# The first norm's second half of scale and shift ahead of chunks 1 and 2 on TensorE, and free banks for layer 1's values

## The chip, the cores and the metric

The kernel runs on one core of a Trainium2 chip. A core has five engines with queues of their own: TensorE (PE: matmuls and transposes, from SBUF into the 8 PSUM banks), VectorE (DVE), ScalarE (ACT), GpSimd (POOL) and SyncE (SP), which here issues the loads of the weights. The metric is the device time of one execution in microseconds (us), median of several runs; less is better.

## The reference, cut to what matters

A decoder trunk of 2 layers on 256 tokens with a model width of 1024. Every sub-layer normalises its input and scales and shifts it by a projection of the condition c:

```
for i in range(DEPTH):                                  # DEPTH = 2
    mod = jax.nn.silu(c) @ ada_w[i] + ada_b[i]          # 1024 x 6144
    sh_a, sc_a, g_a, sh_f, sc_f, g_f = jnp.split(mod[:, None, :], 6, axis=-1)
    h = rms_norm(x, attn_norm[i]) * (1.0 + sc_a) + sh_a
    if i % 2 == 0:
        y = sparse_mixer(h, ...)   # MoBA (8 heads) beside NSA (8 heads, 2 groups)
    else:
        y = diff_mixer(h, ...)     # differential attention, 8 heads
    x = x + g_a * y
    h = rms_norm(x, ffn_norm[i]) * (1.0 + sc_f) + sh_f
    x = x + g_f * ((jax.nn.silu(h @ w_gate) * (h @ w_up)) @ w_down)

def diff_mixer(h, ...):
    q, k, v = jnp.split(h @ w_in, [qk_w, 2 * qk_w], axis=-1)   # 1024 columns each
    # rms_norm and rotary embedding of q and k; v goes on as it is
    # a = softmax(q0 k0) - lam * softmax(q1 k1);  o = a @ v, per head
    return (rms_norm(o, out_norm) * (1.0 - lam_init)) @ w_out
```

## The kernel before, in words

**Products.** Each fp32 product is done as three matmuls of a rounded and a remaining part: `mm3` issues hi x hi, hi x lo and lo x hi into one PSUM bank. A weight comes by DMA in units of 512 KB into one of 5 `raw` buffers (`raw_tile`); `split` (L186 to 188) writes `hi` on ACT (L187) and `lo` on DVE (L188) into one of 5 ring buffers. The activations are kept transposed and split as `bigT` buffers, in two halves of 512 of the 1024 input features each (`hts[0]`, `hts[1]`), both for all 256 tokens.

**Order.** A scheduler sets the order on each engine by its own estimate of times; it prefers what was written first. `weave` mixes several generators of instructions by their weights. `hold` is a list from which each weight unit takes an entry: its split then stands behind the named instructions. `chain`, if it is not empty, ties each matmul behind the one before it, the first behind the name in the list. Neither costs a semaphore wait of its own. SP issues the loads in the order of the program.

**Banks.** `bank_tiles` are the 8 PSUM banks; `banks(...)` gives groups their banks (ACC for accumulations, others for scores, transposes and outputs), and `bank(*group)` takes the next of a group.

**The first norm** (`nsa_first`, L920 and after). `ada_first(0)` multiplies the condition (`cs`) with the first half of scale and shift, 8 loads of 512 KB; the row goes into a bank, is copied out on ACT (L383), transposed back into columns by PE (L387) and finished on DVE (L354, L356: `col`). `out_half(0)` transposes the first half of the normalised x (`xn`, L406, in `norm_T`) and scales, shifts and splits it on ACT (L422, L187) and DVE (L415, L188) into the first `bigT`. The first projection has three chunks of 512, 512 and 280 columns in the banks (0,1), (2,3) and (4,5). `ada_first(1)` takes the second half of scale and shift by 8 loads, whose tiles come from the list `FIRST` and, where that is used up, from the `raw` ring; then come `out_half(1)`, `half(n, 0)` for the three chunks (the matmuls on the first `bigT`), and `half(n, 1)` (those on the second).

**Layer 1** (`diff_proj`, `diff_heads`). Part 0 projects K and Q for the first four heads (`proj2`: kTn, qT), then the values (`proj` with `prep_v`: vm). Part 1 does the same for the other four (kTm, qTm), and runs woven with the heads of part 0. In a head the scores (`kTn,qT`) go into banks 4 and 5, a softmax row is made on DVE (L890) and ACT (L892), two of them are combined on DVE (L1246 to L1250), transposed (L909) and multiplied with the values (`vm,pT`).

Of the kernel before, what the change touches and what calls it, by code (L numbers as in the profile page):

```python
# [17 lines left out]
P = 128  # L18
# [3 lines left out]
NT = S // P  # L22
# [10 lines left out]
RND = 12582912.0  # L33
WARM = 0
NQ = 2


def BOTH(i, j, n):
# [6 lines left out]
def weave(*gens):  # L45

    live = [[g, n, 0] for g, n in gens]
    while live:
        live.sort(key=lambda e: (e[2] + 0.5) / e[1])
        e = live[0]  # L50
        try:
            next(e[0])
            e[2] += 1
        except StopIteration:
            live.remove(e)
# [8 lines left out]
def tile_trunk(ctx: ExitStack, tc: tile.TileContext, x, c, positions, ada_w, ada_b, attn_norm, ffn_norm,  # L64
# [4 lines left out]
    V, A, T, G = nc.vector, nc.scalar, nc.tensor, nc.gpsimd  # L69
# [6 lines left out]
    bank_tiles = [pp.tile([P, 512], F32, name=f"bank{i}") for i in range(8)]  # L76
    bank_at = {}

    def bank(*group):
        i = bank_at.get(group, 0)  # L80
        bank_at[group] = i + 1
        return bank_tiles[group[i % len(group)]]

    ACC, SC, TR, OT, CB = [], [], [], [], []
# [16 lines left out]
    def tmp(shape, tag, bufs, dt=F32):  # L101
        return sp.tile(shape, dt, name=nm(tag), tag=tag, bufs=bufs)
# [8 lines left out]
    chain = []  # L111
# [20 lines left out]
    ident = cp.tile([P, P], F32, name="ident")  # L132
# [58 lines left out]
    hold = []  # L191
# [6 lines left out]
    def raw_tile():  # L198
        return wp.tile([P, 1024], F32, name=nm("raw"), tag="raw", bufs=5)

    FIRST = [("nkv", 2), ("nkv", 2), ("tok4", 2), ("tok4", 2), ("qTm", 1), ("kTm", 1), ("vm", 1), ("kTn", 1),
             ("mod", 2), ("mod", 2), ("qT", 1), ("ada_acc", 2), ("araw", 2), ("araw", 2), None]

    def first_raw():

        if not FIRST:
            return raw_tile()
        at = FIRST.pop(0)
        if at is None:
            return bias  # L210
        if at[0] == "araw":
            return wp.tile([P, 1024], F32, name=nm("araw"), tag="araw", bufs=2)
        return tmp([P, 1024], *at)

    R5 = ("ring",) * 5
    units = dict(first=[], cyc=list(R5), n=0)
# [186 lines left out]

    def norm_T(t, f, xn, b):
        for k in range(4):
            T.transpose(out=b[:, k * P:(k + 1) * P], in_=xn[:, f * 512 + k * P:f * 512 + (k + 1) * P], identity=ident)  # L406

    def norm_out(i, js, t, f, b, ht, behind=None):

        sh, sc = cols[(i, js)], cols[(i, js + 1)]  # L410
        hf = tmp([P, 4, P], "w2k", 4)
        for k in range(4):
            kk = f * 4 + k
            if k % 2:
                v = V.tensor_scalar(out=hf[:, k, :], in0=b[:, k * P:(k + 1) * P], scalar1=sc[:, kk:kk + 1],  # L415
                                    scalar2=sh[:, kk:kk + 1], op0=ALU.mult, op1=ALU.add)
                if behind:
                    after(v, behind)
                ks = slice(k - 1, k + 1)
                h = split(hf[:, ks], ht[0][:, ks, t * P:(t + 1) * P], ht[1][:, ks, t * P:(t + 1) * P])  # L420
            else:
                A.activation(out=hf[:, k, :], in_=b[:, k * P:(k + 1) * P], func=AF.Identity, scale=sc[:, kk:kk + 1],  # L422
                             bias=sh[:, kk:kk + 1])
        return h[1], h[0]
# [82 lines left out]
        yield  # L507
        yield from late(*its)

    def proj(hts, w, c0, n, done):  # L510

        bs = [bank(*ACC) for _ in range(NT)]
        for u in range(4):
            wu, = proj_units(w, c0, n, [u])
            for t in range(NT):
                proj_mm(hts, bs[t][:, 0:n], t, u, wu)
            yield
        yield from done(bs)
# [230 lines left out]
    def prep_v(v):  # L749
        def done(bs):  # L750
            for t in range(NT):
                A.activation(out=v[t], in_=bs[t], func=AF.Copy)
            yield
        return done
# [167 lines left out]
    def nsa_first(hts):  # L922

        w = sp_w_in[0]
        spec = [(1536, 512, (0, 1)), (2048, 512, (2, 3)), (2560, 280, (4, 5))]
        xn = [tmp([P, D], "xn", 2) for _ in range(NT)]

        def out_half(f):
            for t in range(NT):
                b = bank_tiles[6 + t if f or not t else 5]  # L930
                norm_T(t, f, xn[t], b)
                lst[:] = [norm_out(0, 0, t, f, b, hts[f])]

        lst = []

        def half(n, f, wus=None):
            c0, w_, bi = spec[n]
            for e in range(2):
                u = 2 * f + e
                wu = wus[e] if wus else proj_units(w, c0, w_, [u])[0]  # L940
                for t in range(NT):
                    proj_mm(hts, bank_tiles[bi[t]][:, 0:w_], t, u, wu)

        def stats():
            for t in range(NT):
                ss = tmp([P, 2], "ss2", 2)
                for e in range(2):
                    sumsq_x(t, e, ss, xn[t])
                norm_stats(t, ss, xn[t])

        setup_rope()
        ada_first(0, bank_tiles[4], bank_tiles[7])
        stats()
        out_half(0)
        hold[:] = [None] + [lst[0]] * 5
        wus = [proj_units(w, c0, w_, (0, 1)) for c0, w_, _ in spec]
        ada_first(1, bank_tiles[7], bank_tiles[7])
        out_half(1)
        for n in range(3):
            half(n, 0, wus[n])  # L960
        V.memset(bias, 0.0)
        dma(bias[0:12, :], ada_b.rearrange("i (j n) -> (i j) n", j=6))
        setup_small(lst[0])
        for n in range(3):
            half(n, 1)
            yield [bank_tiles[k] for k in spec[n][2]]
# [233 lines left out]
    def diff_proj(hts, part, st):  # L1200
        w = diff_w_in[0]
        qT = tmp([P, 1024], "qT" if part == 0 else "qTm", 1).rearrange("p (k n) -> p k n", k=4)
        kT = tmp([P, 1024], "kTn" if part == 0 else "kTm", 1).rearrange("p (k n) -> p k n", k=4)
        if part == 0:
            vt = tmp([P, NT, 512], "vm", 1)
            v = [vt[:, t, :] for t in range(NT)]
        else:
            v = [tmp([P, 1024], "nkv", 2)[:, 0:512] for _ in range(NT)]
        nrs = tmp([P, NT, 8], "nrs", 2)
        st[part] = (qT, kT, v, nrs)  # L1210
        cs_ = (1024 + part * 512, part * 512)
        dones = (prep_k(kT, 7, fc(5)), prep_q(qT, nrs, 6, 1.0))
        if part == 0:
            yield from proj2(hts, w, cs_, dones)
        else:
            for c0, d in zip(cs_, dones):
                yield from proj(hts, w, c0, 512, d)
        yield from proj(hts, w, 2048 + part * 512, 512, prep_v(v))

    def diff_heads(part, st, oh, ol):  # L1220
        qT, kT, v, nrs = st[part]
# [51 lines left out]
    def first(g, n):  # L1273
        for _ in range(n):
            if next(g, g) is g:
                return
            yield

    def late(*gens):
        for g in gens:  # L1280
            yield from g
# [6 lines left out]
    on = pair()  # L1288
    om = pair()
    nh = nsa_heads(*on)  # L1290
    weave((late(np_, first(nh, 6)), 22), (moba_proj(hts), 20), (ada(0, 2, pin=True), 11))
    hts = new_hts()
    banks([], [0, 1, 2], [4, 5], [6, 7])
    settle()
# [62 lines left out]
```

## Time and profile before

| | |
|---|---|
| median of 3 runs | 755.86 us (754.24 to 756.33) |
| profiled execution | 762.01 us, span 759.9 us |
| mean granted TensorE clock | 0.967 of full speed |
| PE busy | 712.9 us, 94% of the span |
| DVE busy | 505.6 us, 67% |
| ACT busy | 415.1 us, 55% |
| DMA | 159.41 MB, mean 210 GB/s |
| chain that ended last | PE 75%, DVE 8%, DMA 7%, ACT 6% |

The profile is of one execution, which took 6.15 us longer than the median. Busy shares are over the whole span; what holds up the kernel at one place is read from the rows of that place: a row names the engine, the line, the names and shapes of the tiles, and in square brackets how long the engine had stood idle before it and what released it. PEclk is the clock that TensorE was granted, as a share of its full speed.

### The profile page before, as it was taken

How to read it: one execution, taken by the hardware profiler on the slowest of the kernel's cores; microseconds unless marked ns; L12 is line 12 of the kernel's file. 1: busy time of each engine (PE TensorE's matmuls, PEld its weight loads, DVE VectorE, ACT ScalarE, POOL GpSimd, SP SyncE). 2: the span in 40 equal slices, each digit the busy share in tenths (PEclk: the TensorE clock that was granted, in tenths of full speed). 3: DMA queues.
4: the chain of work that ended last, by engine and by line, in shares of the span. 5: the costliest groups of instructions: out<-in, count | busy, mean ns of one | idle time of the engine just before them, and what ended most of it. 6: DMA issues, size and time to landing. Idle time of an engine off the chain costs nothing.

```text
span 759.9 us, 10791 instructions
## 1 busy us (share of the span) xinstructions
PE 712.9 (94%) x3822; PEld 542.6 (71%) x3822; DVE 505.6 (67%) x1078; ACT 415.1 (55%) x813; POOL 40.6 (5%) x131
## 2 busy tenths in 40 slices
PE   4889899899989999999999989998899999999997
PEld 1458666554667888888887768764677888888885
DVE  3556667465676889788854964656777787665642
ACT  3456544587657455655553746666656565555530
POOL 5003111000000000000000030110000000000000
PEclk9598999899999999999999999999899999999999
DMA  9964378036827989999852553207847977556501
GB/s 323 379 206 151 111 267 300 2 118 236 290 95 253 331 291 343 316 309 313 276 181 82 190 199 113 81 1 293 318 138 239 323 261 246 177 184 197 177 25 56
DMA packets 86525, 159.41 MB, mean 210 GB/s; under 512 B 6199, under 2 KB 48316, under 8 KB 86472
## 3 DMA queue, kind: packets, MB, share of 16 engines
q1 hardware_dynamic: 85992, 158.72, 61.2%
q8 instruction: 30, 0.49, 0.3%
q14 instruction: 23, 0.19, 0.1%
q0 software_dynamic: 480, 0.01, 0.0%
HBM read 157.66 MB, written 1.05 MB: 209 GB/s over the span
## 4 chain that ended last, share of the span: by engine, by line
PE 75%; DVE 8%; DMA 7%; ACT 6%; issue 2%; POOL 1%; SPq 0%; DVEq 0%; ACTq 0%
PE bank L115 72%; DMA araw<-in_ada_w_dram 2%; DVE lo L188 2%; PE bank L909 1%; ACT hi L187 1%; DMA tok<-in_ada_w_dram 1%; DMA vm<-in_ada_w_dram 1%; DMA raw<-in_sp_w_out_dram 1%; DMA raw<-in_diff_w_out_dram 1%; PE bank L709 1%; DMA raw<-in_ffn_w_gate_dram 1%; DVE s L890 1%; DVE bigT L188 1%; PE bank L406 1%; ACT bigT L187 1%
## 5 line engine op out<-in xcount | busy, mean ns | idle before, releaser
L188 DVE TENSOR_TENSOR lo<-raw,hi 128x1024 fp32r<-128x1024 f32 x131 | 156.9, 1206 | 76.9 <-ACT hi L187 76.4
L187 ACT ACTIVATE hi<-raw 128x1024 fp32r<-128x1024 f32 x131 | 135.2, 1043 | 81.4 <-PE bank L115 51.6
L115 PE MATMUL bank<-hi,bigT 128*128 128x512 f32 (+1 forms) x472 | 160.8, 410 | 10.9 <-ACT bigT L187 7.1
L115 PE MATMUL bank<-bigT,hi 128*128 128x512 f32 (+1 forms) x400 | 130.9, 380 | 0.0
L115 PEld LDWEIGHTS bank<-hi,bigT 128*128 128x128 f32 x472 | 91.6, 198 | 36.4 <-ACT bigT L187 8.2
L115 PE MATMUL bank<-bigT,lo 128*128 128x256 f32 x368 | 98.5, 281 | 0.0
L115 PE MATMUL bank<-lo,bigT 128*128 128x512 f32 (+1 forms) x236 | 96.0, 407 | 1.6 <-DVE lo L188 1.5
L115 PEld LDWEIGHTS bank<-bigT,hi 128*128 128x128 f32 x400 | 71.7, 189 | 12.7 <-issue 0.7
L115 PEld LDWEIGHTS bank<-bigT,lo 128*128 128x128 f32 x368 | 69.5, 189 | 3.9 <-issue 0.2
L281 DVE SCALAR_TENSOR_TENSOR ada_acc<-araw,cs,ada_acc 128x1024 f32<-128x1024 f32 x46 | 58.8, 1278 | 19.2 <-DMA araw<-in_ada_w_dram 19.2
L115 PEld LDWEIGHTS bank<-lo,bigT 128*128 128x128 f32 x236 | 46.9, 199 | 14.2 <-DVE lo L188 3.8
L890 DVE CUSTOM_DVE_ANT_0 s<-bank,maskc,nrs 128x128 f32<-128x128 f32 (+1 forms) x80 | 29.9, 411 | 29.1 <-PE bank L115 14.4
L892 ACT ACTIVATE s<-s,mx 128x128 f32<-128x128 f32 (+1 forms) x80 | 35.7, 449 | 12.1 <-DVE mx L890 11.5
L618 ACT ACTIVATE w2k<-bank 128x256 f32<-128x256 f32 x64 | 23.9, 378 | 32.9 <-PE bank L115 32.9
L619 DVE TENSOR_TENSOR w2k<-bank,w2k 128x256 f32<-128x256 f32 x64 | 26.6, 417 | 9.7 <-ACT w2k L618 9.7
L115 PE MATMUL bank<-bigT,nkv 128*128 128x256 f32 (+1 forms) x176 | 31.5, 322 | 0.0
L188 DVE TENSOR_TENSOR tok<-raw,tok 128x1024 fp32r<-128x1024 f32 x19 | 23.2, 1221 | 9.1 <-ACT tok L187 9.1
L393 ACT ACTIVATE xn<-xs 128x512 f32<-128x512 f32 x16 | 10.1, 630 | 32.3 <-DVE xs L453 26.5
L187 ACT ACTIVATE nkv<-raw 128x1024 fp32r<-128x1024 f32 x19 | 20.1, 1059 | 13.6 <-PE bank L115 8.1
L115 PEld LDWEIGHTS bank<-bigT,nkv 128*128 128x128 f32 x176 | 25.5, 188 | 2.8
L187 ACT ACTIVATE tok<-raw 128x1024 fp32r<-128x1024 f32 x19 | 20.1, 1058 | 13.2 <-PE bank L115 10.7
L188 DVE TENSOR_TENSOR nkv<-raw,nkv 128x1024 fp32r<-128x1024 f32 x19 | 23.2, 1221 | 5.6 <-ACT nkv L187 5.6
(340 smaller groups left out, 1252.3 us busy)
## 6 DMA issues: line engine op xcount, KB each, us to landing
araw<-in_ada_w_dram SPq DMA_DIRECT2D x50, 512.0 KB, 5.4
raw<-in_ffn_w_gate_dram SPq DMA_DIRECT2D x44, 512.0 KB, 5.2
raw<-in_ffn_w_up_dram SPq DMA_DIRECT2D x44, 512.0 KB, 5.0
raw<-in_ffn_w_down_dram SPq DMA_DIRECT2D x44, 512.0 KB, 5.2
raw<-in_ada_w_dram SPq DMA_DIRECT2D x33, 512.0 KB, 4.8
raw<-in_diff_w_in_dram SPq DMA_DIRECT2D x24, 512.0 KB, 4.6
raw<-in_sp_w_in_dram SPq DMA_DIRECT2D x20, 512.0 KB, 5.8
raw<-in_nsa_cmp_w_dram SPq DMA_DIRECT2D x8, 512.0 KB, 4.0
```

What stands on the lines that cost most here:

```text
L115: ins = T.matmul(o, lhsT=lhsT, rhs=rhs, start=start, stop=stop).ins
L187: i1 = A.activation(out=hi, in_=src, func=AF.Copy)
L188: i2 = V.tensor_tensor(out=lo, in0=src, in1=hi.bitcast(F32), op=ALU.subtract)
L281: ins = V.scalar_tensor_tensor(out=acc, in0=raw, scalar=cs[:, k:k + 1], in1=acc, op0=ALU.mult, op1=ALU.add)
L393: return A.activation(out=junk[:, fs], in_=xs[:, t, fs], func=AF.Square, accum_out=ss[:, f:f + 1])
L406: T.transpose(out=b[:, k * P:(k + 1) * P], in_=xn[:, f * 512 + k * P:f * 512 + (k + 1) * P], identity=ident)
L618: A.activation(out=s[:, f * S:(f + 1) * S], in_=bs[f][:, S:512], func=AF.Copy)
L619: V.tensor_tensor(out=s[:, f * S:(f + 1) * S], in0=bs[f][:, 0:S], in1=s[:, f * S:(f + 1) * S], op=ALU.add)
L709: T.transpose(out=b[:, k * P:(k + 1) * P], in_=src[:, k * P:(k + 1) * P], identity=ident)
L890: V.tensor_tensor_reduce(out=s[:, o:o + n], in0=b[:, o:o + n], in1=maskc[:, S - n:S], scale=nr(t), scalar=3e38, op0=ALU.add, op1=ALU.min, ...
L892: A.activation(out=s[:, o:o + n], in_=s[:, o:o + n], func=AF.Exp, scale=-1.0, bias=mx[:, t:t + 1], accum_out=sm[:, t:t + 1])
L909: T.transpose(out=b[:, k * P:(k + 1) * P], in_=s[:, k * P:(k + 1) * P], identity=ident)
```

## The change

Four edits. The list `FIRST` gets one more entry, so that the last of the 8 loads of `ada_first(1)` has a tile of its own (a buffer that later holds a `bigT`). From chunk QN = 1 on, the matmuls of the first half are chained behind the last transpose of `out_half(1)`, and `hold` is set anew. The values of part 0 in layer 1 go into banks 3 and 5 instead of the next two of the group ACC. A weight in the weave of the first layer's heads is 9 instead of 11. Line numbers below the first edits shift by 1 to 7.

```diff
@@ -33,6 +33,7 @@
 RND = 12582912.0
 WARM = 0
 NQ = 2
+QN = 1
 
 
 def BOTH(i, j, n):
@@ -199,7 +200,7 @@
         return wp.tile([P, 1024], F32, name=nm("raw"), tag="raw", bufs=5)
 
     FIRST = [("nkv", 2), ("nkv", 2), ("tok4", 2), ("tok4", 2), ("qTm", 1), ("kTm", 1), ("vm", 1), ("kTn", 1),
-             ("mod", 2), ("mod", 2), ("qT", 1), ("ada_acc", 2), ("araw", 2), ("araw", 2), None]
+             ("mod", 2), ("mod", 2), ("qT", 1), ("ada_acc", 2), ("araw", 2), ("araw", 2), None, ("bigT", 3)]
 
     def first_raw():
 
@@ -210,7 +211,7 @@
             return bias
         if at[0] == "araw":
             return wp.tile([P, 1024], F32, name=nm("araw"), tag="araw", bufs=2)
-        return tmp([P, 1024], *at)
+        return tmp([P, 2048 if at[0] == "bigT" else 1024], *at)[:, 0:1024]
 
     R5 = ("ring",) * 5
     units = dict(first=[], cyc=list(R5), n=0)
@@ -403,7 +404,8 @@
 
     def norm_T(t, f, xn, b):
         for k in range(4):
-            T.transpose(out=b[:, k * P:(k + 1) * P], in_=xn[:, f * 512 + k * P:f * 512 + (k + 1) * P], identity=ident)
+            q = T.transpose(out=b[:, k * P:(k + 1) * P], in_=xn[:, f * 512 + k * P:f * 512 + (k + 1) * P], identity=ident)
+        return q
 
     def norm_out(i, js, t, f, b, ht, behind=None):
 
@@ -507,9 +509,9 @@
         yield
         yield from late(*its)
 
-    def proj(hts, w, c0, n, done):
-
-        bs = [bank(*ACC) for _ in range(NT)]
+    def proj(hts, w, c0, n, done, bs=None):
+
+        bs = bs or [bank(*ACC) for _ in range(NT)]
         for u in range(4):
             wu, = proj_units(w, c0, n, [u])
             for t in range(NT):
@@ -928,8 +930,9 @@
         def out_half(f):
             for t in range(NT):
                 b = bank_tiles[6 + t if f or not t else 5]
-                norm_T(t, f, xn[t], b)
+                q = norm_T(t, f, xn[t], b)
                 lst[:] = [norm_out(0, 0, t, f, b, hts[f])]
+            return q
 
         lst = []
 
@@ -955,9 +958,13 @@
         hold[:] = [None] + [lst[0]] * 5
         wus = [proj_units(w, c0, w_, (0, 1)) for c0, w_, _ in spec]
         ada_first(1, bank_tiles[7], bank_tiles[7])
-        out_half(1)
+        q = out_half(1)
+        hold[:] = [None] + [lst[0]] * 3
         for n in range(3):
+            if n == QN:
+                chain[:] = [q.ins.name]
             half(n, 0, wus[n])
+        chain[:] = []
         V.memset(bias, 0.0)
         dma(bias[0:12, :], ada_b.rearrange("i (j n) -> (i j) n", j=6))
         setup_small(lst[0])
@@ -1215,7 +1222,7 @@
         else:
             for c0, d in zip(cs_, dones):
                 yield from proj(hts, w, c0, 512, d)
-        yield from proj(hts, w, 2048 + part * 512, 512, prep_v(v))
+        yield from proj(hts, w, 2048 + part * 512, 512, prep_v(v), None if part else [bank_tiles[3], bank_tiles[5]])
 
     def diff_heads(part, st, oh, ol):
         qT, kT, v, nrs = st[part]
@@ -1288,7 +1295,7 @@
     on = pair()
     om = pair()
     nh = nsa_heads(*on)
-    weave((late(np_, first(nh, 6)), 22), (moba_proj(hts), 20), (ada(0, 2, pin=True), 11))
+    weave((late(np_, first(nh, 6)), 22), (moba_proj(hts), 20), (ada(0, 2, pin=True), 9))
     hts = new_hts()
     banks([], [0, 1, 2], [4, 5], [6, 7])
     settle()
```

How the order on the engines changes, at three places (names: number of the tile behind the name).

PE in the first norm, before: the rows around the two transposes of scale and shift (L387) and those of xn (L406), with the matmuls of chunk 2 (banks 4 and 5) on the first bigT ahead of them.

```order
L115 MATMUL bank4_71<-hi54_329,bigT3_104 128x280
L115 MATMUL bank5_72<-hi54_329,bigT3_104 128x280
L115 MATMUL bank5_72<-lo55_330,bigT3_104 128x280
L115 MATMUL bank5_72<-hi54_329,bigT3_104 128x280 x2
L115 MATMUL bank5_72<-lo55_330,bigT3_104 128x280
L115 MATMUL bank5_72<-hi54_329,bigT3_104 128x280
L387 MATMUL bank7_74<-ident_77,w2k63_382 128x128
L406 MATMUL bank7_74<-ident_77,xn11_112 128x128 x4
L115 MATMUL bank0_67<-hi67_533,bigT4_105 128x512
L115 MATMUL bank0_67<-lo68_534,bigT4_105 128x512
```

The same place after; `cs` are the matmuls of scale and shift, the last of them on the new tile.

```order
L116 MATMUL bank7_74<-araw61_365,cs_83 1x256 x4
L116 MATMUL bank7_74<-bias_81,cs_83 1x256 x4
L116 MATMUL bank7_74<-bigT62_376,cs_83 1x256 x4
L388 MATMUL bank7_74<-ident_77,w2k63_382 128x128 x2
L407 MATMUL bank7_74<-ident_77,xn11_112 128x128 x4
L116 MATMUL bank2_69<-hi45_311,bigT3_104 128x512
L116 MATMUL bank2_69<-lo46_312,bigT3_104 128x512
L116 MATMUL bank2_69<-hi45_311,bigT3_104 128x512 x2
L116 MATMUL bank2_69<-lo46_312,bigT3_104 128x512
L116 MATMUL bank2_69<-hi45_311,bigT3_104 128x512
```

The transposes have moved in front of the matmuls of chunks 1 and 2 (banks 2 to 5); only chunk 0 is ahead of them.

PE at the end of the K and Q projections of layer 1, before: behind the last unit of K and Q (tok, bank 4) comes the values' first (bank 0).

```order
L115 MATMUL bank4_71<-tok4711_3922,bigT396_2125 128x512
L115 MATMUL bank4_71<-tok4712_3923,bigT396_2125 128x512
L115 MATMUL bank4_71<-tok4711_3922,bigT396_2125 128x512 x2
L115 MATMUL bank4_71<-tok4712_3923,bigT396_2125 128x512
L115 MATMUL bank4_71<-tok4711_3922,bigT396_2125 128x512
L115 MATMUL bank0_67<-hi754_4225,bigT395_2124 128x512
L115 MATMUL bank0_67<-lo755_4226,bigT395_2124 128x512
L115 MATMUL bank0_67<-hi754_4225,bigT395_2124 128x512 x2
L115 MATMUL bank0_67<-lo755_4226,bigT395_2124 128x512
```

After: behind the same unit come matmuls in banks 5 and 3.

```order
L116 MATMUL bank4_71<-tok4711_3922,bigT396_2125 128x512
L116 MATMUL bank4_71<-tok4712_3923,bigT396_2125 128x512
L116 MATMUL bank4_71<-tok4711_3922,bigT396_2125 128x512 x2
L116 MATMUL bank4_71<-tok4712_3923,bigT396_2125 128x512
L116 MATMUL bank4_71<-tok4711_3922,bigT396_2125 128x512
L116 MATMUL bank5_72<-qTm739_4163,bigT395_2124 128x512
L116 MATMUL bank5_72<-kTm740_4164,bigT395_2124 128x512
L116 MATMUL bank5_72<-qTm739_4163,bigT395_2124 128x512 x2
L116 MATMUL bank5_72<-kTm740_4164,bigT395_2124 128x512
L116 MATMUL bank5_72<-qTm739_4163,bigT395_2124 128x512
L116 MATMUL bank3_70<-hi742_4181,bigT396_2125 128x512
L116 MATMUL bank3_70<-lo743_4182,bigT396_2125 128x512
```

The values no longer take a bank of K and Q, and part of them stands further up, ahead of these rows.

PE at the heads of part 0, before: scores of a head (`kTn,qT`), transposes, products with the values (`vm,pT`), and a projection of part 1 behind them.

```order
L115 MATMUL bank2_69<-hi823_4537,bigT396_2125 128x512
L115 MATMUL bank4_71<-kTn686_3876,qT685_3875 128x128
L115 MATMUL bank4_71<-kTn686_3876,qT685_3875 128x256
L115 MATMUL bank5_72<-kTn686_3876,qT685_3875 128x128
L115 MATMUL bank5_72<-kTn686_3876,qT685_3875 128x256
L909 MATMUL bank7_74<-ident_77,s758_4248 128x128 x3
L115 MATMUL bank4_71<-kTn686_3876,qT685_3875 128x128
L115 MATMUL bank4_71<-kTn686_3876,qT685_3875 128x256
L115 MATMUL bank3_70<-vm687_3877,pT769_4290 128x128 x3
L115 MATMUL bank5_72<-kTn686_3876,qT685_3875 128x128
L115 MATMUL bank5_72<-kTn686_3876,qT685_3875 128x256
L909 MATMUL bank6_73<-ident_77,s777_4340 128x128 x3
```

After: the scores of three heads stand in a row, the transposes of two heads behind them.

```order
L116 MATMUL bank4_71<-kTn686_3876,qT685_3875 128x256
L116 MATMUL bank5_72<-kTn686_3876,qT685_3875 128x256
L116 MATMUL bank4_71<-kTn686_3876,qT685_3875 128x128
L116 MATMUL bank4_71<-kTn686_3876,qT685_3875 128x256
L116 MATMUL bank5_72<-kTn686_3876,qT685_3875 128x128
L116 MATMUL bank5_72<-kTn686_3876,qT685_3875 128x256
L116 MATMUL bank4_71<-kTn686_3876,qT685_3875 128x128
L116 MATMUL bank4_71<-kTn686_3876,qT685_3875 128x256
L116 MATMUL bank5_72<-kTn686_3876,qT685_3875 128x128
L116 MATMUL bank5_72<-kTn686_3876,qT685_3875 128x256
L911 MATMUL bank7_74<-ident_77,s758_4248 128x128 x3
L911 MATMUL bank6_73<-ident_77,s777_4340 128x128 x3
```

The matmuls of part 1 that stood between the heads now stand ahead of them or behind all four.

## Rows read from the trace of the kernel before

**Rows 1.** A window of a feed-forward stage: busy us (x instructions), clock, DMA

```profile
600.00:720.00 120.00, 120.00 (x632) 102.30 (x631) 79.65 (x97) 63.71 (x91) 0.00 (x0) 1.00 0.67 221
```

**Rows 2.** What PE waited for from 20 to 62: us, times, longest

```profile
PE bank L115 <- ACT bigT L187: 5.6, 2, 3.0
PE bank L387 <- ACT w2k L383: 0.5, 1, 0.5
PE bank L406 <- DVE col L354: 0.3, 1, 0.3
PE bank L387 <- DVE col L354: 0.3, 1, 0.3
```

**Rows 3.** Timeline of PE, first norm: start, us, instruction [idle before <- releaser]

```profile
52.06 0.66 PE L406 MATMUL bank<-ident,xn 128*128 128x128 f32 x4 [0.26 <-DVE col L354]
55.34 0.80 PE L115 MATMUL bank<-hi,bigT 128*128 128x512 f32 x1 [2.62 <-ACT bigT L187]
```

**Rows 4.** Windows of the first norm: length, PE, PEld, DVE, ACT, POOL, clock

```profile
55.30:62.00 6.70, 6.66 (x20) 5.42 (x20) 2.48 (x8) 3.20 (x7) 0.00 (x0) 0.56 0.62 227
44.34:46.66 2.32, 2.32 (x11) 1.69 (x9) 2.32 (x3) 1.06 (x1) 0.00 (x0) 1.00 0.75 238
48.58:50.39 1.81, 1.81 (x17) 1.81 (x15) 0.77 (x1) 1.81 (x2) 0.00 (x0) 1.00 0.95 284
```

**Rows 5.** The last load of scale and shift: issue on SP, wait, landing

```profile
29.67 0.37 SPq L367 DMA_DIRECT2D raw<-in_ada_w_dram  x1
...
SPq L367 <- DMA ada_acc<-in_ada_w_dram: 0.9, 1, 0.9
...
raw<-in_ada_w_dram SPq DMA_DIRECT2D x1, 512.0 KB, 7.6
```

**Rows 6.** Timelines of DVE and ACT in the first norm

```profile
44.15 0.91 DVE L961 MEMSET bias<- 128x1024 f32 x1 [1.00 <-PE bank L115]
...
49.49 2.17 ACT L271 ACTIVATE ada_acc<-bias,ident 128x1024 f32<-128x1024 f32 x2
...
56.77 0.42 ACT L187 ACTIVATE bigT<-w2k 128x256 fp32r<-128x256 f32 x1 [0.17 <-DVE w2k L415]
```

**Rows 7.** Timelines of PE and ACT at the values' projection of layer 1

```profile
445.77 0.50 PE L115 MATMUL bank<-hi,bigT 128*128 128x512 f32 x1 [2.63 <-ACT w2k L686]
...
440.86 1.06 ACT L187 ACTIVATE araw<-raw 128x1024 fp32r<-128x1024 f32 x1 [3.05 <-DMA raw<-in_diff_w_in_dram]
```

**Rows 8.** Window behind that wait

```profile
446.00:452.00 6.00, 6.00 (x20) 4.79 (x20) 3.07 (x5) 2.64 (x6) 3.16 (x15) 0.72 0.78 279
```

**Rows 9.** Heads of layer 1: timelines of PE and DVE, then DVE's groups (mean ns)

```profile
477.91 0.93 PE L115 MATMUL bank<-kTn,qT 64*128 64x128 f32 x8
479.96 0.92 PE L115 MATMUL bank<-kTn,qT 64*128 64x128 f32 x4 [0.64 <-DVE mx L890]
480.81 0.94 PE L115 MATMUL bank<-vm,pT 128*128 128x128 f32 x6
...
475.98 0.17 DVE L1246 RECIPROCAL sm<-sm 128x2 f32<-128x2 f32 x1 [1.03 <-ACT s L892]
476.52 0.73 DVE L1250 SCALAR_TENSOR_TENSOR s<-s,sm,s 128x128 f32<-128x128 f32 x2
...
L890 DVE CUSTOM_DVE_ANT_0 s<-bank,maskc,nrs 128x256 f32<-128x256 f32 x4 | 1.8, 478 | 0.0
L890 DVE CUSTOM_DVE_ANT_0 s<-bank,maskc,nrs 128x128 f32<-128x128 f32 x5 | 1.6, 348 | 2.2 <-PE bank L115 2.2
```

**Rows 10.** Waits of PE elsewhere, and windows with little work on PE

```profile
220.78 0.97 PE L115 MATMUL bank<-nkv,bigT 128*128 128x512 f32 x3 [1.44 <-ACT bigT L187]
...
525.08 0.44 PE L319 MATMUL bank<-ident,w2k 128*128 128x128 f32 x2 [1.52 <-ACT w2k L317]
...
525.00:529.00 4.00, 3.92 (x33) 1.19 (x33) 2.21 (x12) 0.31 (x3) 0.00 (x0) 0.57 0.37 109
533.00:536.00 3.00, 1.24 (x11) 0.53 (x11) 2.72 (x14) 0.40 (x2) 0.00 (x0) 0.94 0.96 382
```

**Rows 11.** The page's group of the accumulations of scale and shift

```profile
L281 DVE SCALAR_TENSOR_TENSOR ada_acc<-araw,cs,ada_acc 128x1024 f32<-128x1024 f32 x46 | 58.8, 1278 | 19.2 <-DMA araw<-in_ada_w_dram 19.2
```

## The prediction

> **What bounds the kernel now.** I read the windows first, then the waits of TensorE (PE), then its rows in order of time around the waits that the change touches. In the long feed-forward stages PE is busy without a gap: 120.00 of 120.00 us at the full granted clock [rows 1]. So work that ends earlier ahead of such a stage brings the end forward by as much, and I look for time only where PE waits or runs at its lower clock. The change touches two such places.
>
> *The first norm.* Between 20 and 62 us the largest wait of PE is for the second half of the normalised input, bigT [rows 2]. PE finishes everything of the first half, transposes the second half at 52.06, and then stands for 2.62 us until ScalarE (ACT) and VectorE (DVE) have scaled and split it [rows 3]. [...]
>
> *Layer 1.* After the last matmuls of the K and Q projections PE waits 2.63 us for ACT to empty a bank for the values' projection, and again the clock is low afterwards: 0.72 over 6 us, 1.7 us lost [rows 7, 8]. ACT is late because it had waited for a load and then did four weight splits (440.86 and after) ahead of the evacuations.
>
> **The change, part by part.**
>
> *1. Transposes of the second half before chunks 1 and 2.* Today the chain "accumulated shift and scale, copied out, two transposes, two columns, transposes of xn" lies at the very end of the first half, with waits of 0.5, 0.3 and 0.3 us, 1.1 in all [rows 2]. In the new order only chunk 0 runs before it; the 48 matmuls of chunks 1 and 2 come behind. PE's work ahead of the second half is the same, so it ends at 52.72 (the transposes at 52.06 and their 0.66 [rows 3]), less the old waits, plus the new ones. I take the new ones as 0.5 for the copy as now, 0.55 for the column, which in the new order comes behind the clearing of bias (0.91 us at 44.15 [rows 6]) and one split on DVE, and 0.25 for the second: 1.3 us. So PE is done with the first half at 52.72 - 1.1 + 1.3 = 52.9. Is bigT ready then? From the end of the transposes to the last split today is 57.19 - 52.72 = 4.5 us (56.77 + 0.42 [rows 6]); in the new order two gate rows (2.17 us together [rows 6]) also stand in front on ACT. That is 6.7 us. Behind the transposes PE has 24 matmuls of 512 columns and 24 of 280: 11 of the first kind take 2.32 us and 17 of the second 1.81 [rows 4], those at the edges counted, so the 48 take at least 24 x 0.21 + 24 x 0.106 = 7.6 us. bigT is ready 0.9 us or more ahead of need. The wait of 2.62 goes, and with it the 2.9 us at the lower clock: 55.34 - 52.9 + 2.9 = 5.3 us gained. What would be late next are the splits of the second half's weights: they are now held behind the norm too, but DVE has these 7.6 us for four splits and four halves of the norm, so I cost that at nothing, and at 1 us if they slip.
>
> *2. A tile of its own for the last load.* Its load is issued at 29.67, having waited 0.9 us for the completion of another, not for a buffer, and lands 7.6 us later, at 37.3 [rows 5]. In the new order it stands at the same place of SP's queue. In the new order the matmuls on it lie behind chunk 0 and the loads before it, by my count some 4 us later: nothing gained or lost. It leaves a ring buffer free one turn earlier, which nobody waits for.
>
> *3. Weight 9 for 11 in the weave.* Two accumulations of the shift and scale on DVE (1.28 us each [rows 11]) slip into the head phase, where PE waits little. From 0 to +1, I take +0.5.
>
> *4. Values of layer 1 on banks 3 and 5.* These are free, so 18 of the 48 matmuls run before the K and Q projections are done and the rest right behind. That takes away 2.63 + 1.7 = 4.3 us. But the matmuls come earlier than the heads can begin, and PE runs out of other work to put between the heads: in the new order the score products of the heads stand one behind the other, with the filler (72 matmuls) behind them. Then DVE sets the pace: four heads have 8 softmax rows of 0.348 and 8 of 0.478, 6.6 us; two combinations at about 1.3 each (from 475.98 to the end of the row of 476.52) must also be done before the last product with the values, 2.6; and at the ends stand one head's scores (0.93), its transposes (about 0.5, from 0.66 for four in rows 3) and products with the values (0.94): 11.6 us [rows 9]. PE has of its own in it 4 x 0.93 + 2 x 0.5 + 0.94 = 5.7, so it idles 5.9 us. The 0.64 us that it waits among the heads today [rows 9] are in these. Net: 5.9 - 4.3 - 0.6 = +1.0 us. If the softmax rows overlap more than I think and half of the idle goes, it is -2.0; if the clock falls in the block and stays down as long as after the first norm, +1.0 + 2.9 = +3.9. I take +1.0: the pieces of idle are short ones (a product waits for one softmax row), like those that did not bring the clock down (1.44 us before 220.78); the nearest that did were 1.52 us in one piece (then 0.57 over 4 us), and a stretch with 1.24 busy of 3 us, where the mean is already 0.94 [rows 10].
>
> *Sum.* -5.3 + 0 + 0.5 + 1.0 = -3.8. The profiled execution took 762.01 us (span 759.9), 6.15 above the median of 755.86; I carry the difference over to the median: 755.86 - 3.8 = 752.0, rounded.
>
> **The rivals.**
>
> *A. The clock falls in the first norm's new chain.* The 1.3 us of new waits lie together with a few transposes at 43 to 45 us. Against a fall: no piece is over 0.6. For it: the 3 us with 1.24 busy [rows 10] had two idles of 0.9. Then most of chunks 1 and 2 run at half until the clock is back, and as after the wait of today 2.9 us are lost. The gain shrinks to 2.4: 752.0 + 2.9 = 754.9.
>
> *B. The heads cost nothing.* Half of the idle goes or the scheduler's order lets the DVE run ahead: -2.0 for +1.0, 749.0.
>
> *C. The bunched heads make it slower.* For it: 5.7 busy of 11.6 us is half, and 1.24 of 3 was enough for a fall. If the clock drops at their start, their own 5.7 us double, of which the idle hides a part at most where DVE paces: up to +5.7, and +2.9 behind them: 1.0 + 5.7 + 2.9 = 9.6 at that place, and -5.3 + 0.5 + 9.6 = +4.8, 760.7. The point from which the kernel is slower than before is a loss of 4.8 us in layer 1. Against it: the DVE paces, so a slower PE fills its own idle first. [...]
>
> *D. The transposes do not come earlier.* If the last load's data or the columns were late (it lands 4 us ahead of its use), PE would wait there for what it now waits for later, and there is no gain in the first norm: 755.9 + 0.5 + 1.0 = 757.4.
>
> **How the numbers follow.** The forecast has 0.42, A 0.22, B 0.18, C 0.08, D 0.05, and A together with a fall after the heads (752.0 + 2.9 + 2.9 = 757.8) 0.05. What a measurement of this kernel can tell from no change is 0.3%, 2.3 us: faster is below 753.6. The forecast's own width is some 1.5 us to both sides, so about 0.38 of its 0.42, all of B and 0.04 of A are faster: 0.60. Slower is above 758.1: C and a part of D and of the last: 0.10. The rest, 0.30, is no change that can be told. The range from 748.8 to 757.0 holds the forecast, A and most of B.
>
> **What would show it.** Right: PE's row for the last of the eight loads directly ahead of the transposes at about 43 to 45 us, no wait for bigT at 53, clock 1.00 from 53 on; second half's first matmul 2 to 2.5 us earlier. In layer 1 no wait for w2k at 443, but PE busy about half over 11 us from about 472 with waits for DVE's softmax, then 48 fillers without a gap. Wrong: a granted clock of 0.50 behind 45 us (A) or in and after the heads (C); a wait for the loads before 43 us (D). The forecast also fails if the second half waits for weight splits (lo) at 53 us by more than 1 us.

## The result, and the profile after

The changed kernel takes 747.96 us (median of 5 runs, 744.81 to 752.87) against 756.0 before: a ratio of 0.9895, 95% interval [0.986, 0.9929], 5.4 to 10.6 us less. Forecast were 752.0 us and a range from 748.8 to 757.0, so the median lies 0.8 us below the range. Measured twice more, with 12 runs each, it had 750.5 us (ratio 0.9929 [0.9898, 0.996]) and 749.28 us (0.9928 [0.9903, 0.9953]); these two medians lie inside the range. By the ratios the three medians are 5.4 to 7.9 us better than before, where 3.8 were forecast; 3.8 lies outside the interval of the first measurement and inside those of the repeats. Ratios and intervals leave out the few executions that lie over 1.5% above the fastest of their kernel.

The profiled execution of the changed kernel took 752.87 us with a span of 750.8 us, 9.1 us less than the span of before. Cut at five matmuls that both programs have, named in the first column, the difference lies here (us; the columns give the length of each stretch, and each boundary, given in the time of before, is the start of a matmul of PE in the two timelines):

| stretch of PE | before | after | difference |
|---|---|---|---|
| first norm: first matmul on bigT (24.47) to the first `raw,od` (90.91) | 66.44 | 61.38 | -5.1 |
| NSA and MoBA: to the feed-forward input, `nkv,bigT` (220.78) | 129.87 | 127.40 | -2.5 |
| feed-forward 0 and layer 1's heads: to `nkv,pT` (520.30) | 299.52 | 299.24 | -0.3 |
| shift and scale, out projection: to `nkv,bigT` (564.78) | 44.48 | 43.07 | -1.4 |
| feed-forward 1: to the end | 195.1 | 195.2 | 0 |

The timeline of PE in the first norm after (start, us, instruction, the idle before it and what ended it) answers to [rows 3]:

```profile
41.65 0.61 PE L116 MATMUL bank<-bigT,cs 128*1 128x256 f32 x8
42.77 0.33 PE L388 MATMUL bank<-ident,w2k 128*128 128x128 f32 x1 [0.50 <-ACT w2k L384]
43.78 0.33 PE L388 MATMUL bank<-ident,w2k 128*128 128x128 f32 x1 [0.68 <-DVE col L355]
44.36 0.66 PE L407 MATMUL bank<-ident,xn 128*128 128x128 f32 x4 [0.25 <-DVE col L355]
...
53.67 0.50 PE L116 MATMUL bank<-hi,bigT 128*128 128x512 f32 x1
```

The last load's matmuls (the row at 41.65) stand directly ahead of the transposes, the new waits are 0.50, 0.68 and 0.25 us (1.4; forecast 1.3), and the second half begins at 53.67 without a wait, 1.67 us earlier than at 55.34 (forecast 2 to 2.5). Behind it the windows show the clock (length, busy us and instructions of PE, PEld, DVE, ACT and POOL, granted clock, DMA share, GB/s), first the window that answers to [rows 4], then three around the heads of layer 1:

```profile
53.00:62.00 9.00, 9.00 (x43) 7.39 (x42) 6.84 (x15) 5.68 (x10) 0.15 (x1) 1.00 0.81 273
466.00:470.00 4.00, 1.39 (x10) 0.92 (x8) 2.66 (x15) 3.62 (x12) 0.00 (x0) 1.00 0.00 0
471.00:477.00 6.00, 6.00 (x27) 3.98 (x25) 4.41 (x22) 4.92 (x19) 0.00 (x0) 0.50 0.01 3
478.00:482.00 4.00, 4.00 (x19) 3.26 (x19) 2.94 (x11) 3.52 (x13) 2.09 (x7) 1.00 0.01 2
```

From 53 to 62 the clock is now full. In layer 1 the wait of [rows 7] is gone, and the four heads now stand in one block. The timeline of PE there answers to [rows 9]:

```profile
439.99 0.39 PE L116 MATMUL bank<-qTm,bigT 128*128 128x512 f32 x1
...
465.14 0.93 PE L116 MATMUL bank<-kTn,qT 64*128 64x128 f32 x8
467.30 1.32 PE L116 MATMUL bank<-kTn,qT 64*128 64x128 f32 x8 [1.23 <-DVE mx L892]
470.25 1.77 PE L116 MATMUL bank<-kTn,qT 64*128 64x128 f32 x8 [1.63 <-DVE mx L892]
471.95 1.60 PE L911 MATMUL bank<-ident,s 128*128 128x128 f32 x6
473.43 1.65 PE L116 MATMUL bank<-vm,pT 128*128 128x128 f32 x6
475.01 1.66 PE L116 MATMUL bank<-kTn,qT 64*128 64x128 f32 x8
476.60 1.50 PE L116 MATMUL bank<-vm,pT 128*128 128x128 f32 x6
477.85 1.63 PE L116 MATMUL bank<-ada_acc,bigT 128*128 128x512 f32 x6
```

From 465.14 to 477.85 are 12.7 us (forecast 11.6; 12.3 and 12.0 in the profiles of the repeats). PE idles 1.23 and 1.63 us behind VectorE's softmax rows, 2.9 in all where 5.9 were forecast. The granted clock falls to 0.50 at about 471 and is back at 478, when the block is over; meanwhile the products with the values take 1.50 to 1.65 us instead of 0.94 [rows 9].

The second row of the table is what I had not forecast. In front of it stands one accumulation of scale and shift on VectorE (the line of [rows 11]). First the rows of DVE, POOL, DVE again and PE around 93 us before:

```profile
93.19 1.27 DVE L281 SCALAR_TENSOR_TENSOR ada_acc<-araw,cs,ada_acc 128x1024 f32<-128x1024 f32 x1
...
93.35 1.18 POOL L157 TENSOR_SCALAR rs_w<-ss 128x16 f32<-128x16 f32 x1 [15.63 <-DVE ss L687]
...
98.15 1.29 DVE L742 TENSOR_TENSOR tok<-tok,rs_y 128x512 f32<-128x512 f32 x2 [1.35 <-POOL rs_y L160]
99.36 1.22 DVE L188 TENSOR_TENSOR lo<-raw,hi 128x1024 fp32r<-128x1024 f32 x1
...
100.63 0.50 PE L115 MATMUL bank<-lo,bigT 128*128 128x512 f32 x1 [1.10 <-DVE lo L188]
```

Then those after:

```profile
88.36 0.20 POOL L158 TENSOR_SCALAR rs_w<-ss 128x16 f32<-128x16 f32 x1 [16.62 <-DVE ss L689]
...
93.22 1.22 DVE L189 TENSOR_TENSOR lo<-raw,hi 128x1024 fp32r<-128x1024 f32 x1
96.03 1.27 DVE L282 SCALAR_TENSOR_TENSOR ada_acc<-araw,cs,ada_acc 128x1024 f32<-128x1024 f32 x1
```

Before, the first of GpSimd's twelve small operations (an inverse square root on 16 columns) begins while VectorE does the accumulation, and takes 1.18 us. VectorE idles 1.35 us for the result of the twelve (rs_y; 1.13 after), and its lo stands behind that. After, the accumulation stands behind, the same operation takes 0.20 us, VectorE's lo comes 4.86 us behind its start (6.01 before), and PE's wait of 1.10 us is gone. That is 1.1 of the 2.5 us of this stretch. The rest is not located: in the profiles of the two repeats the stretch takes 127.9 and 129.3 us, so single profiles differ by as much.

### The profile page after: what moved, and what is told of

The parts are those of the page before. It is cut to its first block, busy times and chain, and to the rows that moved or that the text cites. A ratio compares the mean times of both kernels' runs of the same rounds, so it can differ in the third digit from the quotient of the medians.

```text
span 750.8 us, 10789 instructions
## 1 busy us (share of the span) xinstructions
PE 706.4 (94%) x3822; PEld 540.6 (72%) x3822; DVE 504.5 (67%) x1078; ACT 414.6 (55%) x813; POOL 40.8 (5%) x131
## 3 DMA queue, kind: packets, MB, share of 16 engines
HBM read 157.66 MB, written 1.05 MB: 211 GB/s over the span
## 4 chain that ended last, share of the span: by engine, by line
PE 77%; DMA 8%; DVE 6%; ACT 5%; issue 3%; SPq 1%; DVEq 0%; ACTq 0%
PE bank L116 73%; PE bank L911 2%; DMA araw<-in_ada_w_dram 2%; DMA bias<-in_ada_w_dram 2%; DMA raw<-in_ada_w_dram 1%; DMA raw<-in_sp_w_in_dram 1%; DVE lo L189 1%; DMA xs<-in_x_dram 1%; DMA raw<-in_ffn_w_gate_dram 1%; PE bank L711 1%; ACT hi L188 1%; DVE ada_acc L282 1%; PE bank L407 1%; ACT bigT L188 1%; DVE bigT L189 1%
## 5 line engine op out<-in xcount | busy, mean ns | idle before, releaser
L116 PE MATMUL bank<-hi,bigT 128*128 128x512 f32 (+1 forms) x472 | 154.0, 397 | 5.2 <-ACT bigT L188 4.4
L116 PEld LDWEIGHTS bank<-hi,bigT 128*128 128x128 f32 x472 | 89.2, 192 | 26.0 <-ACT bigT L188 5.3
L116 PE MATMUL bank<-lo,bigT 128*128 128x512 f32 (+1 forms) x236 | 93.8, 398 | 0.5 <-DVE lo L189 0.4
L116 PEld LDWEIGHTS bank<-lo,bigT 128*128 128x128 f32 x236 | 45.3, 192 | 13.4 <-DVE lo L189 3.9
```

The costliest lines, as they stand in the source:

```text
L116: ins = T.matmul(o, lhsT=lhsT, rhs=rhs, start=start, stop=stop).ins
```

## The experiments

The experiments ran in three groups, each beside the kernel before: e1 to e4_no_banks (before: 756.1 us); a_again, f1, e5 and e6 (756.08); e4_again, a_third, w10 and w7 (755.52). Gains and losses in us are the ratio's distance from 1 times that median.

**e1_first_norm: the first norm's part alone.** The kernel before with these edits, and those that hand the last transpose q on:

```diff
-             ("mod", 2), ("mod", 2), ("qT", 1), ("ada_acc", 2), ("araw", 2), ("araw", 2), None]
+             ("mod", 2), ("mod", 2), ("qT", 1), ("ada_acc", 2), ("araw", 2), ("araw", 2), None, ("bigT", 3)]
...
+        q = out_half(1)
+        hold[:] = [None] + [lst[0]] * 3
...
+            if n == QN:
+                chain[:] = [q.ins.name]
```

> The kernel before with the first norm's part alone (own tile for the last load, transposes ahead of chunks 1 and 2, hold set anew). Theory: the gain of the first norm is what the two traces show at 85 to 91 us, 4.8 to 5.0 us, so about 751 (ratio 0.9935), with no wait for bigT at 53 and the wait for a weight's lo of 1.1 us at 100 still there. Rival (the whole gain of 8 us hangs on the first norm, because everything after it is shifted and loads and splits fall better): 748, and no wait for lo at about 96.

Measured 752.71 us, ratio 0.9953 [0.9931, 0.9976]: 1.8 to 5.2 us less. In its profile the first norm's stretch is 61.40 us, as in the changed kernel; GpSimd's operation still stands beside the accumulation and takes 1.17 us, and the wait for lo is still there (rows of POOL and PE):

```profile
87.92 1.17 POOL L158 TENSOR_SCALAR rs_w<-ss 128x16 f32<-128x16 f32 x1 [16.61 <-DVE ss L689]
...
95.20 0.51 PE L116 MATMUL bank<-lo,bigT 128*128 128x512 f32 x1 [1.10 <-DVE lo L189]
```

The forecast's -5.3 lies a tenth of a us beyond the interval; of 5.0 us in the stretch, 3.6 arrive at the end in the median. The rival that everything hangs on the first norm is out.

**e2_banks: the values on banks 3 and 5 alone.**

```diff
-        yield from proj(hts, w, 2048 + part * 512, 512, prep_v(v))
+        yield from proj(hts, w, 2048 + part * 512, 512, prep_v(v), None if part else [bank_tiles[3], bank_tiles[5]])
```

> The kernel before with layer 1's values on banks 3 and 5 alone. Theory: 4.3 us of wait and low clock go at the values, 3 to 4 us of wait and low clock come at the bunched heads; net 0 to -0.5, about 755.6 (ratio 0.999 to 1.000). Rival (the place gives most of what the forecast missed): -3 to -4 us, about 752.5. My forecast had +1.0, 757.

Measured 759.71 us, ratio 1.0061 [1.0031, 1.0092]: 2.3 to 7.0 us more, against both theories; my forecast's +1.0 had the sign. In its profile PE waits again and again in the heads, the last time 1.46 us, and the clock is 0.52 over 10 us. Rows of the timeline:

```profile
475.68 1.32 PE L115 MATMUL bank<-kTn,qT 64*128 64x128 f32 x8 [1.63 <-DVE mx L890]
...
484.29 1.65 PE L115 MATMUL bank<-vm,pT 128*128 128x128 f32 x6 [1.46 <-ACT od L1260]
```

The window over the end of this block:

```profile
478.00:488.00 10.00, 8.32 (x30) 6.29 (x31) 6.87 (x30) 7.46 (x31) 0.53 (x3) 0.52 0.00 1
```

**e3_weave: weight 9 for 11 alone.**

```diff
-    weave((late(np_, first(nh, 6)), 22), (moba_proj(hts), 20), (ada(0, 2, pin=True), 11))
+    weave((late(np_, first(nh, 6)), 22), (moba_proj(hts), 20), (ada(0, 2, pin=True), 9))
```

> The kernel before with weight 9 for 11 alone. Theory: one accumulation of 1.27 us on VectorE leaves the stretch in front of a weight's lo on which TensorE waits 1.1 us at 100, and later ones go where nobody waits: -1 to -2.5 us, about 754 (ratio 0.997 to 0.9985). Rival (no effect or a small loss, as forecast, and the difference between the traces there comes from the shift in time by the first norm): 755.9 to 756.9, the wait of 1.1 us still there.

Measured 752.83 us, ratio 0.9961 [0.9938, 0.9983]: 1.3 to 4.7 us less, where I had forecast half a us more. The wait for lo is gone, without the first norm's part, and GpSimd's operation is short (rows of POOL and PE):

```profile
92.92 0.20 POOL L157 TENSOR_SCALAR rs_w<-ss 128x16 f32<-128x16 f32 x1 [15.62 <-DVE ss L687]
...
103.48 0.74 PE L115 MATMUL bank<-hi,bigT 128*128 128x512 f32 x2 [1.05 <-ACT hi L187]
```

In this execution PE waits 1.05 us a little later instead, for the hi of a load that came late (ACT had idled 4.39 us for it), and the stretch of NSA and MoBA is only 0.6 us shorter than before (129.26 us). The execution took 761.28 us, over 8 above the median, so its profile does not show where the median's gain lies. In the three profiles of the changed kernel the same wait for hi is nothing, 0.55 and 0.95 us.

**e4_no_banks and e4_again: the changed kernel without the banks**, the edit of e2 taken back.

> The changed kernel with layer 1's values back on the next two banks of the accumulation group. Theory: as the changed kernel, at most 0.5 us slower: 748 to 748.5; the wait of 2.6 us for w2k at the values is back with a low clock behind it, and the heads have their filler and the full clock. Rival (the banks give what the forecast missed): 751 to 752.

> The changed kernel without the banks (values of layer 1 on the group's next two banks) a second time, now beside the changed kernel in the same call. If the banks cost 1 to 3 us, it lies that much below the changed kernel: ratio to before 0.990 to 0.991 against 0.992 to 0.993. If they are worth nothing, the two agree within 1 us.

Measured 747.88 us (0.9903 [0.9878, 0.9929]) and 747.64 us (0.9904 [0.9872, 0.9935]). Beside them the changed kernel had, as a_again and a_third,

> The changed kernel unaltered, beside the others on this chip. If the banks cost what the first experiments say alone (+2.3 to +7.0 us), it must lie 2 to 5 us above the changed kernel without them (747.9): 750 to 753. If the banks are worth nothing beside the other edits, 747 to 749.

> The changed kernel a third time, for the comparison with the kernel without the banks in this call: 749 to 751 if the first two measurements (747.96, 750.5) are samples of one spread.

750.5 and 749.28 us. In the group that had both, the version without the banks has the lower median by 1.6 us, but the intervals overlap, and the first measurement of the changed kernel (747.96, ratio 0.9895) lies as low as the version without. So beside the other edits the banks cost 0 to 3 us, and nothing at all is not excluded. The version without them is below the kernel before for certain; that it is below the changed one is not shown. The wait of layer 1 for w2k is back in it (2.01 us in e4_no_banks, 2.66 in e4_again).

**f1_filler: projection matmuls between the heads again.** The scores of heads 1, 2 and 3 are tied behind matmuls of part 1, and a fixed order of heads (h) and projections (p) takes the place of their weave:

```diff
+    PIN = {1: (512, 3, 1), 2: (2560, 3, 0), 3: (2560, 1, 1)}
...
+                fills[(c0, u, t)] = proj_mm(hts, bs[t][:, 0:n], t, u, wu)
...
+                                  None if part else fills.get(PIN.get(hh)))
...
+    for ch in 'pphpppppppphhpppppphhhhhpp':
+        next(gs[ch], None)
```

> The changed kernel with the scores of heads 1, 2 and 3 of layer 1's part 0 tied behind projection matmuls of part 1 (Q's last, values' first and second token half), so that filler stands between the heads again. Theory: the bunched heads cost 3 us of idle and a stretch of some 7 us at the lower clock (3.4 us lost); with filler both go: 3 to 6 us below the changed kernel, 742 to 746, no 0.50 in the clock between 440 and 500. Rival (the head stretch costs nothing, since idle and low clock cover each other): the same as the changed kernel, 748.

Measured 751.39 us, ratio 0.9934 [0.9908, 0.996], not to be told from the changed kernel's 750.5. The windows show the filler at the first heads and the clock at the later ones:

```profile
466.00:496.00 30.00, 28.96 (x158) 21.97 (x156) 18.80 (x91) 19.99 (x71) 3.00 (x13) 1.00 0.04 14
499.00:508.00 9.00, 9.00 (x46) 5.10 (x48) 7.50 (x42) 6.41 (x28) 0.00 (x0) 0.50 0.03 4
```

The heads of part 0 run at full clock with 1.0 us of idle in 30, but the filler is then missing at the heads of part 1, where PE waits 0.52 and 0.86 us at 496 to 498 and the clock is at 0.50 for 9 us. In this order the filler is one stock that covers either place.

**e5_no_tile: without the own tile.**

```diff
-             ("mod", 2), ("mod", 2), ("qT", 1), ("ada_acc", 2), ("araw", 2), ("araw", 2), None, ("bigT", 3)]
+             ("mod", 2), ("mod", 2), ("qT", 1), ("ada_acc", 2), ("araw", 2), ("araw", 2), None]
```

> The changed kernel without the own tile for the last load of scale and shift (it takes a raw buffer as before); chain and hold as in the changed kernel. Theory: the load waits for the completion of another load, not for a buffer, so nothing changes: the same as the changed kernel, 747.5 to 748.5. Rival (the raw buffer it frees lets a weight of the first chunks in earlier, or the load itself comes earlier): 1 to 3 us slower, with a wait for a load or a weight's lo between 40 and 55.

Measured 751.11 us, ratio 0.9922 [0.9888, 0.9957], beside 750.5 of the changed kernel: the tile is worth nothing that can be told, as forecast. Its first norm is 61.29 us.

**e6_no_chain: without the chain and the new hold**, the rest as in the changed kernel.

```diff
-        hold[:] = [None] + [lst[0]] * 3
...
-            if n == QN:
-                chain[:] = [q.ins.name]
```

> The changed kernel without the chain behind the second half's transposes and without the new hold; own tile, banks and weight 9 as in the changed kernel. Theory: the first norm's gain goes, with the wait of 2.6 us for bigT and the low clock behind it: 3.5 to 5 us slower than the changed kernel, 751.5 to 753. Rival (the gain comes from the tile, or the shift by the weave): 748 to 749.

Measured 758.4 us, ratio 1.0045 [1.0015, 1.0074], 7.9 us above the changed kernel beside it (more than the theory's 3.5 to 5). The wait for bigT is back:

```profile
51.12 0.50 PE L115 MATMUL bank<-hi,bigT 128*128 128x512 f32 x1 [2.19 <-ACT bigT L187]
...
478.27 1.65 PE L115 MATMUL bank<-vm,pT 128*128 128x128 f32 x6 [1.77 <-ACT od L1260]
```

The window behind the first of these waits is at full clock:

```profile
51.12:58.00 6.88, 6.88 (x32) 5.55 (x33) 3.04 (x9) 4.01 (x9) 0.00 (x0) 1.00 0.33 105
```

So the loss is not the first norm's alone. In this profile (755.25 us, the shortest of the 12 runs) the first norm takes 60.43 us, no longer than in the changed kernel, since its start ran at a mean clock of 0.80 (23.75 to 37), the changed kernel's, by the times of its matmuls, slower (last paragraph). The stretch from 220 to 520 takes 303.44 us, 4.2 more than in the changed kernel: the block of four heads is 15.2 us long instead of 12.7, with the wait of 1.77 us at 478.27 that the changed kernel does not have.

**w10_no_banks and w7_no_banks: weights 10 and 7**, in e4's kernel.

```diff
-    weave((late(np_, first(nh, 6)), 22), (moba_proj(hts), 20), (ada(0, 2, pin=True), 9))
+    weave((late(np_, first(nh, 6)), 22), (moba_proj(hts), 20), (ada(0, 2, pin=True), 10))
```

The other run has 7 in the same place.

> As the changed kernel without the banks, but with weight 10: in the order of the engines the third accumulation then stays ahead of the weight's lo on VectorE and the two matmuls that spread the accumulated row stay ahead of the heads on TensorE, as with 11; only the last two accumulations move a little. Theory (the gain of the weight comes from these two places): nothing of the 3 us is had, 750.5 to 752, the wait of 1.1 us for lo at 95 is there. Rival (the gain comes from spreading the accumulations as such, in proportion to the weight): half of it, 749 to 749.5.

> As the changed kernel without the banks, with weight 7: the third accumulation and the two matmuls stand behind as with 9, the later ones further behind. Theory: as with 9, 747.5 to 748.5, no wait for lo at 95. Rival (in proportion): 745.5 to 746.5.

Measured 754.63 us (0.9992 [0.9966, 1.0019]) and 756.11 us (1.0 [0.9975, 1.0024]) beside 747.64 with weight 9. Both theories for 7 fall, and with 10 more is lost than theirs. Weight 11 in the same kernel is e1_first_norm: 0.9953, between 9 and 10. The stretch of NSA and MoBA takes 126.63 us with 9 (e4_again), 133.64 with 10 and 135.31 with 7. With 10 GpSimd's operation stands beside the accumulation again and takes 1.17 us, and another accumulation stands in the middle of the softmax of the compressed keys; rows of POOL, DVE and PE of that kernel:

```profile
84.28 1.17 POOL L158 TENSOR_SCALAR rs_w<-ss 128x16 f32<-128x16 f32 x1 [16.64 <-DVE ss L689]
...
133.66 1.28 DVE L282 SCALAR_TENSOR_TENSOR ada_acc<-araw,cs,ada_acc 128x1024 f32<-128x1024 f32 x1
...
136.61 0.69 PE L1144 MATMUL bank<-ident,scc 128*128 128x128 f32 x2 [3.85 <-DVE scc L1140]
```

The same row with weight 9:

```profile
131.65 0.44 PE L1144 MATMUL bank<-ident,scc 128*128 128x128 f32 x2 [2.35 <-DVE scc L1140]
```

PE waits 1.5 us longer, about the accumulation's 1.28. With the wait for lo that is 2.6 of the 7.0 us; the rest is not located. With 7 it is a later place: an accumulation stands ahead of VectorE's clearing of the bank for the next loads of scale and shift, PE waits for that, and behind it for one of the loads (rows of DVE and PE).

```profile
153.29 1.28 DVE L282 SCALAR_TENSOR_TENSOR ada_acc<-araw,cs,ada_acc 128x1024 f32<-128x1024 f32 x1
...
154.69 0.27 DVE L326 MEMSET bank<- 128x256 f32 x1
...
155.01 2.34 PE L116 MATMUL bank<-raw,cs 128*1 128x256 f32 x40 [1.66 <-DVE bank L326]
...
162.03 0.61 PE L116 MATMUL bank<-raw,cs 128*1 128x256 f32 x8 [1.27 <-DMA raw<-in_ada_w_dram]
```

So the weight is no quantity of which less is better: it decides which accumulation stands ahead of which short chain.

## Why the prediction was wrong

**The step that failed is part 3**, the weight: "From 0 to +1, I take +0.5". Alone it measured -2.9 (-4.7 to -1.3), and beside the chain, from e1_first_norm to e4_no_banks, -3.8. I had asked only where the moved accumulations go (into the heads, "where PE waits little") and not what they leave: beside the row at 93.19 GpSimd's operation took 1.18 us instead of 0.20, and behind that chain stood the lo for which PE waited 1.10 us at 100. That is what the traces show of the term: 1.1 of the 2.9. The rest is not located. One candidate was not tried by itself: the two matmuls that spread the accumulated row stand among the first layer's heads with 11 and 10 (at 148.93 before) and behind them with 9 and 7 (150.69 after). With -2.9 for +0.5 the sum would have been 755.86 - 5.3 - 2.9 + 1.0 = 748.7.

*Part 1* was right in mechanism and in the traces (new waits 1.4 us for 1.3, stretch shorter by 5.1 for 5.3); end to end alone it gave 3.6, less than forecast. Its term of 2.9 us for the low clock behind the wait, which rival A and the cost of a fall after the heads take over, is an estimate, (1 - 0.56) x 6.7 from [rows 4]: no run shows it as a time of its own. What the runs show in its place is a clock that is not low in every execution: behind e6's wait of 2.19 us it stayed at 1.00. Rival A did not come: with pieces of 0.50, 0.68 and 0.25 us the clock was 1.00 from 43 to 53 us. *Part 2* was right (e5_no_tile; 0). Rival D is out.

*Part 4* had the sign and the shape: no wait for w2k, heads behind each other, PE idle on softmax rows. Its choice that the clock does not fall in the block was wrong; it fell in the profiles of the changed kernel (0.50 from 471 to 477 us) and of e2_banks (0.52 from 478 to 488). In the former it was back when the block ended, and the block took 12.7 us for 11.6. The forecast's sum for PE's own work counts one group of products with the values (0.94) where the block has two; what it put down as idle was in good part matmuls at the low clock. The 1.7 us of low clock that the edit was to save at the values are also not always there: behind the wait of 2.01 us in e4_no_banks the clock is 1.00. Alone the banks cost 4.6 us (2.3 to 7.0), more than the +1.0, and the point of 4.8 from which rival C decides lies inside that interval; beside the other edits they cost 0 to 3 us.

*What stays open.* The parts alone give -3.6, -2.9 and +4.6, that is -1.9; together -5.4 to -7.9. The chain and the weight do add up (-6.5 alone, -7.3 together in e4_no_banks); the term that changes is the banks. The profiles show where: in the two kernels with the banks and without the chain, e2_banks and e6_no_chain, the last products of the block of heads stand directly behind the ones before them and wait for ACT to copy these out (1.46 us at 484.29, 1.77 at 478.27), and the block takes 15.0 and 15.2 us. With the chain, a head's scores stand between the two, that wait is absent, and the block takes 12.0 to 12.7 (the changed kernel three times, e5_no_tile). So 2.3 to 3.2 us of what the banks cost alone depend on the chain, and with them a part of the chain's 8.8 us beside the other edits (by the ratios, from +3.4 without to -5.4 with it; 3.6 alone). That the scheduler's estimates, shifted by the earlier first norm, give the other order is likely, but not tried. The -1.4 us of the stretch from 520 to 565 belongs to no edit: there the clock falls in some executions and not in others (below).

## What to carry to other kernels

Before costing a moved instruction by its length, look at what stood behind it on its engine, and behind that on the others: what it leaves can be worth more than what it takes. Matmuls used as filler between dependent heads are one stock, so an edit that uses them earlier has to be charged for the place where they are missed. And a weight in a scheduler's mix is searched point by point, each with its trace, since its neighbours (10 and 7 beside 9) can lose all of the gain. An edit measured alone has only the price that it has in that order: the banks cost 4.6 us alone and 0 to 3 beside the chain.

## What the runs showed of the hardware

**GpSimd's operation takes longer beside VectorE's accumulation.** The TENSOR_SCALAR on 16 columns takes 0.20 or 0.21 us, and 1.17 or 1.18 us where VectorE does the accumulation of 1.26 to 1.28 us at the same time: so at that place in the kernel before, e1_first_norm, e2_banks and w10_no_banks (accumulation beside it) against the changed kernel, e3_weave, e4_again and w7_no_banks (none). The changed kernel shows both in one trace: 0.20 us at 88.36, and where another accumulation has just begun (rows of DVE and POOL)

```profile
122.04 1.26 DVE L282 SCALAR_TENSOR_TENSOR ada_acc<-araw,cs,ada_acc 128x1024 f32<-128x1024 f32 x1
...
122.19 1.18 POOL L158 TENSOR_SCALAR rs_w<-ss 128x16 f32<-128x16 f32 x1 [30.22 <-DVE ss L689]
```

The rows show the two times, not what makes the difference.

**The clock differs between executions at the same place.** Behind the wait of 1.52 us at 525.08 the kernel before had a mean clock of 0.57 over 4 us [rows 10]. The same matmul of the changed kernel waits as long:

```profile
517.34 0.44 PE L320 MATMUL bank<-ident,w2k 128*128 128x128 f32 x2 [1.53 <-ACT w2k L318]
```

but the window behind it is at full speed:

```profile
517.00:521.00 4.00, 3.66 (x45) 1.49 (x45) 2.41 (x14) 1.07 (x5) 0.00 (x0) 1.00 0.39 123
```

and in a_again, the same program, it is low again:

```profile
518.00:522.00 4.00, 3.76 (x32) 1.17 (x32) 2.34 (x13) 0.47 (x3) 0.00 (x0) 0.58 0.29 67
```

Nor does the length of the wait alone decide. Behind the wait of 2.63 us for w2k in layer 1 the clock of before was 0.72 [rows 8]; e1_first_norm waits 3.10 us at the same place, and the clock is full:

```profile
441.64 0.50 PE L116 MATMUL bank<-hi,bigT 128*128 128x512 f32 x1 [3.10 <-ACT w2k L688]
...
441.60:447.60 6.00, 5.96 (x26) 4.95 (x27) 3.34 (x5) 2.91 (x6) 2.96 (x15) 1.00 0.84 300
```

The first stretch of dense matmuls ran at about 0.50 in e4_no_banks and with many more matmuls at full speed in e4_again, the same program:

```profile
24.70:37.00 12.30, 12.30 (x53) 5.78 (x52) 7.07 (x23) 4.95 (x9) 0.12 (x1) 0.52 1.06 375
24.70:37.00 12.30, 12.27 (x82) 7.01 (x86) 7.77 (x26) 6.26 (x12) 0.12 (x1) 1.00 1.06 375
```

Their first norms took 61.23 and 56.91 us: 4.3 us between two executions at one place. (In the profile of the changed kernel the column of the clock reads 1.00 in this window, but only 51 matmuls ran in it, and its two on `w2k,ones` took 2.07 us together, as in the kernel before at 0.50, where e4_again took 1.12: by these times the clock was low there too.) That is why single profiles differ by more than the edits here, and why the comparisons rest on medians of 5 to 12 runs.
